# A decoder layer with its tile places and its instruction orders written out as tables

## The chip, the core and the metric

The kernel runs on one core of one Trainium2 chip. The metric is the time on the device in microseconds (us); with a single core, the slowest core is that core. The engines are TensorE (PE in the profile; its weight loads are PEld), VectorE (DVE), ScalarE (ACT), GpSimd (POOL) and SyncE (SP), which only issues loads and stores here.

## The reference

One layer of a hybrid decoder on 512 tokens of width 1024, all in float32:

```python
u = rms_norm(h, ln_mix_pre)
proj = einsum('bsd,de->bse', u, w_in)       # q, k, v of two branches, q of the third, three gates
qa, ka, va, qb, kb, vb, qm, gl = split(proj)
y_swa = swa_sink_attention(qa, ka, va, sinks, rel_bias)   # window 128, 8 heads over 2
y_sb  = stick_breaking_attention(qb, kb, vb)              # 8 heads
y_mem = memory_cross_attention(qm, *split(einsum(rms_norm(mem, ln_mem), w_mem_kv)))  # 256 rows
g = sigmoid(gl)                                           # 3 x 1024
merged = g[0]*(y_swa @ w_branch_swa) + g[1]*(y_sb @ w_branch_sb) + g[2]*(y_mem @ w_branch_mem)
h = h + rms_norm(merged @ w_out, ln_mix_post)
u = rms_norm(h, ln_ffn_pre)
a = silu(u @ w_gate) * (u @ w_up)                         # width 2816
h = h + rms_norm(a @ w_down, ln_ffn_post)
```

## The kernel before

**Products.** Each float32 matrix is split into a high and a low part, `hi` and `lo`. The split is one copy on ScalarE (L137) and one subtraction on VectorE (L138), in `split`; a product is then three matmuls, hi x hi, hi x lo and lo x hi (`mm3`, L169 to L171). The large projections also use a scheme with seven block products p1 to p7 in place of eight. Its sums of weight blocks are made while they are loaded: a first plain load from SyncE fills a tile, and a second load, issued on GpSimd, accumulates into it (`q_issue`, L446, for the gates; `g_plus`, L1224, for gate/up; `dn_issue`, L1364 and L1367, for the down projection). The splits of the weights wait for these loads.

**Streams.** Two objects of class `Stream` hold the work of TensorE as a list of units, `dn` up to the branches and `fs` for the feed-forward part. A unit is one load of weights, one split and a row of matmuls (24 of 256 columns in a gate/up unit). When a unit begins, `ahead` writes the load for four or five units further on and the split for three further on; attention, softmax, gates and norms are written between the pieces of the stream, by their estimated times.

**What sets the order.** The source writes the instructions in that order, but what each engine's queue holds in the end is decided by the scheduler of the Tile framework, which moves instructions past each other on an engine by its own model of when their inputs are ready. Some edges are pinned by `after`, which adds a dependency without a semaphore: all functions of one ScalarE table behind the table's load (`fn`, `table`), the splits behind the copies of `q_end`, and the splits, factors and joins of the first gate/up units behind each other (`behind`, `ordered`). The first stage alone is written under a manual schedule. Each engine then takes its queue in order.

**Where tiles live.** The SBUF and PSUM buffers come from pools that turn round: `ckp` with 73 tiles of 128 x 512 float32, `sm` with 16 small ones, `wp` with four each of raw, hi and lo weight tiles of 128 x 1024, `cst` for constants. PSUM has eight banks, two in pool `psd` and six in `psa`. At the end of the branches `wp` and `cst` are closed and the pool `fp`, with nine load buffers and four hi and lo tiles each, takes their room.

**Places that the prediction speaks of.** They are these, in order of time:
- `q_end` (L540): when the products of a gate's block are ready in PSUM, ScalarE copies the bank out, for p1, p5, p6 and p7, and the bank is used again. The tile is `gq2p` for the third gate (MEM).
- `out_load` and `out_split`: the sixteen 256 KB pieces of `w_out` are loaded on SyncE into tiles `wo00` to `wo17` (L1067, two per step of the loop over `outs`), and split on ScalarE and VectorE into `wo00h` and so on.
- `turn` and `place`: the normalized rows are transposed in PSUM (`pt`), and the right-hand factors B11, B21, T1, N2, N22, T3 and T4 of the gate/up products are written from them (`place`, L1153 and L1154). For the first two row tiles `turn` also keeps a copy of both halves, `ur` (L1171).
- `dn_issue`: the loads of the down projection's weights. For p3 a tile `bp` is loaded for each k (L1372), and for p7 another load accumulates into it on GpSimd (L1367).
- `dn_half` (its last lines L1400 to L1409) and `rstd_small` (L1078 to L1083): the last norm, on each half row of the output, and the stores.

Of the kernel before, what the change touches and what calls it, by code (L numbers as in the profile page):

```python
# [2 lines left out]

# [1 line left out]

# [12 lines left out]
P = 128  # L18
# [10 lines left out]
SPLIT_AHEAD = 3  # L29
QM_FIRST = 3  # L30
WARM = 10


class Stream:
# [70 lines left out]

@with_exitstack
def tile_kernel(ctx, tc, a):
    nc = tc.nc

    base = ctx.enter_context(tc.tile_pool(name="base", bufs=1))  # L110
    ckp = ctx.enter_context(tc.tile_pool(name="ckp", bufs=73))
    sm = ctx.enter_context(tc.tile_pool(name="sm", bufs=16))
    psd = ctx.enter_context(tc.tile_pool(name="psd", bufs=2, space=bass.MemoryType.PSUM))
    psa = ctx.enter_context(tc.tile_pool(name="psa", bufs=6, space=bass.MemoryType.PSUM))
    drm = ctx.enter_context(tc.tile_pool(name="drm", bufs=1, space=bass.MemoryType.DRAM))

    first = ExitStack()
    wp = first.enter_context(tc.tile_pool(name="wp", bufs=4))
    cst = first.enter_context(tc.tile_pool(name="cst", bufs=1))

    def ck(name, dt=F32):
        return ckp.tile([P, 512], dt, tag="ck", name=name)

    def small(name, n=4):
        return sm.tile([P, 8], F32, tag="s", name=name)[:, :n]

    def dps(name):
        return psd.tile([P, 512], F32, tag="d", name=name)

    def aps(name):  # L130
        return psa.tile([P, 512], F32, tag="a", name=name)

    st = {}

# [10 lines left out]

    def w_load(src, n):
        uid[0] += 1
        raw = wp.tile([P, 1024], F32, tag="raw", name=f"raw{uid[0]}")
        nc.sync.dma_start(raw[:, :n], src)
        return raw  # L150

    def w_split(raw, n):
        uid[0] += 1
        hi = wp.tile([P, 1024], F32R, tag="hi", name=f"hi{uid[0]}", bufs=4)
        lo = wp.tile([P, 1024], F32R, tag="lo", name=f"lo{uid[0]}", bufs=4)
# [51 lines left out]


    def const(name, shape, pool=cst):
        t = pool.tile(shape, F32, name=f"c_{name}")  # L210
# [5 lines left out]
    ones = cst.tile([P, P], F32, name="ones")  # L216
    nc.vector.memset(ones[:, :], 1.0)

    def rsqrt(r, v, t, ss):
# [8 lines left out]
    def rstd_of(name, acc, n, bank):  # L228


        if acc.shape[1] > n:
            nc.gpsimd.tensor_tensor(acc[:, :n], acc[:, :n], acc[:, n : 2 * n], op=ALU.add)
        ps = bank(f"ss_{name}")
        mm(ps[:, :n], ones[:, :], acc[:, :n], True, True)
        rb = cst.tile([P, n], F32, name=f"rb_{name}")
# [5 lines left out]
        rs = cst.tile([P, n // P], F32, name=f"rs_{name}")  # L241
        nc.gpsimd.dma_start(rs[:, :], row[:, :].rearrange("o (t p) -> (o p) t", p=P))
        return rs, rb

# [96 lines left out]

        return gen

    v_all = cst.tile([P, NT * 640], F32, name="v_all")

    def own_values(t):
        return v_all[:, t * 640 + P : (t + 1) * 640]
# [345 lines left out]
            add_branch(b)  # L693

    xraw = []
    xg = cst.tile([P, 544], F32, name="xg")
    g_pre, g_mem = xg[:, S : S + KC], xg[:, S + KC : S + 2 * KC]
    g_neg = cst.tile([P, KC], F32, name="g_neg")

    def load_x(k0, k1):  # L700
        for k in range(k0, k1):
# [14 lines left out]

    FIRST = 3
    PIECE = ((0, 2), (2, 5), (5, 8))
    raws = [wp.tile([P, 1024], F32, tag="raw", name=f"raw_first{i}") for i in range(FIRST)]
    his = [wp.tile([P, 1024], F32R, tag="hi", name=f"hi_first{i}", bufs=4) for i in range(FIRST)]  # L720
    los = [wp.tile([P, 1024], F32R, tag="lo", name=f"lo_first{i}", bufs=4) for i in range(FIRST)]

    def first_load(eng, p):
        k0, k1 = PIECE[p]
# [4 lines left out]
        sl = slice(PIECE[p][0] * P, PIECE[p][1] * P)  # L729
        split(raws[i][:, sl], his[i][:, sl], los[i][:, sl])  # L730

    with tc.manual_schedule():

        idle = cst.tile([P, 512], BF16, name="idle")
        nc.vector.memset(idle[:, :], 0.0)
        pw = dps("warm")
        for i in range(WARM):
# [42 lines left out]
    pin[:] = [first_table]  # L780

    ident = const("ident", [P, P], base)
    sinks = cst.tile([P, 8], F32, name="sinks")
    nc.sync.dma_start(sinks[:, :], a["sinks"].to_broadcast([P, 8]))

    nmf = const("negm", [P, P])
    identb = cst.tile([P, P], BF16, name="identb")
    nc.gpsimd.tensor_copy(identb[:, :], ident[:, :])
    negm = cst.tile([P, P], BF16, name="negmb")
# [371 lines left out]
    def turn(t, tmp):  # L1161
        pt = [aps(f"ut{t}{h}") for h in range(2)]
        for h in range(2):
            for k in range(4):
                nc.tensor.transpose(pt[h][:, k * P : (k + 1) * P], tmp[h][:, k * P : (k + 1) * P], ident[:, :])
        turned[t] = pt
        if t < 2:
            turned[t] = [ck(f"ur{t}{h}") for h in range(2)]
            for h in range(2):
                place(("B11", "B21")[h], t, pt[h])  # L1170
                nc.scalar.copy(turned[t][h][:, :], pt[h][:, :])  # L1171
# [24 lines left out]

    HF = NFF // 2
    NCH = (HF + 1) // 2
    aq = {(i, j): [ck(f"aq{i}{j}{c}") for c in range(NCH)] for i in range(2) for j in range(2)}
    sq = [ck(f"sq{c}") for c in range(NCH)]  # L1200
    sr = [ck(f"sr{c}") for c in range(NCH)]

    PROD = ("p1", "p5", "p6", "p3", "p7", "p2", "p4")
    AHEAD_A = 3
# [12 lines left out]

    def g_raw(n, key, i, j):
        uid[0] += 1
        gw[(n, key)] = fp.tile([P, 1024], F32, tag="raw", name=f"gw{uid[0]}")  # L1220
        nc.sync.dma_start(gw[(n, key)][:, :], g_src(n, i, j))

    def g_plus(n, key, i, j):
# [117 lines left out]
    keep = {}  # L1341
    out1 = {}
    gain_out = []
    ssd = [small(f"ssd{t}", 2) for t in range(NT)]
    held = []

    def wsrc(j, h, k):
# [5 lines left out]
    def dn_issue(p, c):  # L1353

        j, h = {"p1": (0, 0), "p5": (0, 1), "p6": (1, 1), "p3": (1, 1), "p7": (0, 1), "p2": (1, 0), "p4": (1, 0)}[p]
        ks = tiles_of(c)
        if p in ("p1", "p5", "p4"):
            n = 512 * len(ks)
            src = a["w_dn"][:, h, j * HF + ks[0] : j * HF + ks[-1] + 1].rearrange("p k n -> p (k n)")
            if p == "p1":  # L1360
                rr[c] = fp.tile([P, 1024], F32, tag="raw", name=f"r{c}")
                nc.sync.dma_start(rr[c][:, :n], src)
            else:
                nc.gpsimd.dma_start(rr[c][:, :n], src, accum_op=ALU.add)  # L1364
        elif p == "p7":
            for k, t in zip(ks, rb[("p3", c)]):
                nc.gpsimd.dma_start(t[:, :], wsrc(j, h, k), accum_op=ALU.add)  # L1367
# [101 lines left out]
    gpost = bcast("g_post")  # L1469
    gfpre = bcast("g_fpre")  # L1470
    dn.until(f"branch{MEM}")
    first.close()
    fp = ctx.enter_context(tc.tile_pool(name="fp", bufs=9, reuse_waits="tile"))

    def f_split(raw, n):
        uid[0] += 1
        hi = fp.tile([P, 1024], F32R, tag="hi", name=f"hi{uid[0]}", bufs=4)
        lo = fp.tile([P, 1024], F32R, tag="lo", name=f"lo{uid[0]}", bufs=4)
# [18 lines left out]
    def load_at(i, fn, *args):  # L1497
        fs.units[i]["load"].append(lambda: fn(*args))
# [26 lines left out]
    def go(to):  # L1525
        while fs.at < to:
            fs.piece()
# [43 lines left out]
    go(len(seq))  # L1571
    table("natural_log_exp_and_others")
    go(len(fs.units))


def _buckets():
# [86 lines left out]
```

## Time and profile before

| what | before |
|---|---|
| median of 3 runs | 788.07 us (787.36 to 788.13) |
| the profiled execution | 787.54 us |
| its span | 785.7 us |
| instructions in it | 12,335 |
| busy PE / DVE / ACT / POOL | 776.3 / 595.4 / 469.3 / 123.2 us |
| granted clock of TensorE | 0.999 |
| moved by DMA | 128.61 MB, 164 GB/s |

The time of an execution is a little longer than its span, here by 1.8 us, which lies before the first and behind the last instruction that the profile counts. Busy time is the time in which an engine executes an instruction. TensorE's matmuls overlap, so one has a busy time longer than the distance to the next. A window is a stretch of the span; the wait view adds up the idle time of an engine by what ended it. In a row of the timeline stand the start, the duration, the engine, the line, the operation with what it writes and reads, and in brackets the idle time before it with what ended that.

### The profile page before, as it was taken

To read this page: it belongs to the slowest core of one execution; us is meant where nothing else is said; L and a number is where in the kernel's file an instruction comes from. 1 tells how busy PE (TensorE), PEld (TensorE's weight loads), DVE (VectorE), ACT (ScalarE), POOL (GpSimd) and SP (SyncE) were. 2 spreads that over 40 slices of the span, in tenths; PEclk is the share of its full clock that TensorE was granted. 3 is DMA by queue.
4 is the path that set the end of the run, shared out by engine and by line. 5 is a ranking of instruction groups with operands and counts; after the bars stand their busy time and mean duration, and the time that the engine had idled before them with its cause. 6 is when DMAs were issued, how large, how long until landed. Compare 5 with 4: busy or idle time off the path is not lost.

```text
span 785.7 us, 12335 instructions
## 1 busy us (share of the span) xinstructions
PE 776.3 (99%) x4638; PEld 682.2 (87%) x4638; DVE 595.4 (76%) x942; ACT 469.3 (60%) x837; POOL 123.2 (16%) x142
## 2 busy tenths in 40 slices
PE   9999999999999999999999999999999999999996
PEld 6899887788888888887888899999999999888885
DVE  6995876686877757876855599867677777898797
ACT  7663676686577666657633577455554455666673
POOL 0203400002011111321261000100000000215200
PEclk9999999999999999999999999999999999999999
DMA  8444923265449794369849418987666651949802
GB/s 301 132 138 121 314 88 108 81 190 124 89 100 206 178 208 139 54 170 250 304 162 255 92 47 219 260 220 191 186 180 183 186 155 54 222 107 239 184 1 108
DMA packets 44220, 128.61 MB, mean 164 GB/s; under 512 B 5248, under 2 KB 6832, under 8 KB 44160
## 3 DMA queue, kind: packets, MB, share of 16 engines
q1 hardware_dynamic: 30480, 85.21, 32.8%
q0 software_dynamic: 13248, 42.22, 27.8%
q8 instruction: 36, 0.59, 0.3%
q10 hardware_dynamic: 432, 0.39, 0.1%
q14 instruction: 24, 0.20, 0.1%
HBM read 120.98 MB, written 4.72 MB: 160 GB/s over the span
## 4 chain that ended last, share of the span: by engine, by line
PE 93%; DMA 2%; DVE 2%; issue 1%; ACT 1%; POOL 0%; DVEq 0%; SPq 0%; ACTq 0%; POOLq 0%
PE gx L169 5%; PE gx L171 5%; PE gx L170 5%; PE gy L171 3%; PE gy L169 3%; PE gy L170 3%; PE x L171 3%; PE x L170 3%; PE x L169 3%; PE br L169 2%; PE br L170 2%; PE br L171 2%; PE mx L171 2%; PE mx L170 2%; PE mx L169 2%; PE g1p L169 2%
## 5 line engine op out<-in xcount | busy, mean ns | idle before, releaser
L137 ACT CAST hi<-gw 128x1024 fp32r<-128x1024 f32 x77 | 79.9, 1048 | 92.7 <-DVE gw L1242 39.6
L138 DVE TENSOR_TENSOR lo<-raw,hi 128x1024 fp32r<-128x1024 f32 (+2 forms) x82 | 99.9, 1219 | 46.2 <-ACT hi L137 45.7
L138 DVE TENSOR_TENSOR lo<-gw,hi 128x1024 fp32r<-128x1024 f32 x77 | 93.5, 1223 | 36.2 <-ACT hi L137 36.2
L137 ACT CAST hi<-raw 128x1024 fp32r<-128x1024 f32 (+2 forms) x82 | 85.2, 1042 | 43.4 <-PE pv L171 13.0
L1224 POOL DMA_DIRECT2D gw<-in_w_gu x27 | 23.3, 883 | 196.4 <-DMA gw<-in_w_gu 91.3
L870 DVE TENSOR_TENSOR_SCAN bw<-br,bw 128x512 f32<-128x512 f32 (+3 forms) x32 | 24.4, 808 | 17.0 <-ACT bw L194 17.0
L137 ACT CAST hi<-r 128x1024 fp32r<-128x1024 f32 (+1 forms) x24 | 23.6, 982 | 19.8 <-PE y L171 5.3
L446 POOL DMA_DIRECT2D raw<-in_w_g x24 | 20.7, 862 | 93.2 <-DVE lo L138 74.2
L170 PE MATMUL x<-lo,lh 128*128 128x512 f32 x88 | 34.2, 389 | 0.0
L169 PE MATMUL x<-hi,lh 128*128 128x512 f32 x88 | 34.2, 389 | 0.0
L171 PE MATMUL x<-hi,ll 128*128 128x512 f32 x88 | 34.1, 389 | 0.0
L138 DVE TENSOR_TENSOR lo<-r,hi 128x1024 fp32r<-128x1024 f32 (+1 forms) x24 | 27.1, 1130 | 3.7 <-ACT hi L137 3.6
L137 ACT CAST hi<-bp 128x512 fp32r<-128x512 f32 x33 | 19.3, 620 | 13.4 <-PE y L171 4.8
L138 DVE TENSOR_TENSOR lo<-bp,hi 128x512 fp32r<-128x512 f32 x33 | 22.7, 721 | 6.0 <-ACT hi L137 5.8
L169 PE MATMUL gx<-B11h,hi 128*128 128x256 f32 x88 | 25.1, 285 | 0.2 <-ACT B11h L1153 0.2
L169 PE MATMUL gx<-T4h,hi 128*128 128x256 f32 x88 | 25.0, 285 | 0.0
L169 PE MATMUL gy<-N22h,hi 128*128 128x256 f32 x88 | 25.0, 284 | 0.0
L171 PE MATMUL gy<-N22h,lo 128*128 128x256 f32 x88 | 25.0, 284 | 0.0
L171 PE MATMUL gw<-B21h,lo 128*128 128x256 f32 x88 | 25.0, 284 | 0.0
L170 PE MATMUL gx<-B11l,hi 128*128 128x256 f32 x88 | 25.0, 284 | 0.0
L170 PE MATMUL gw<-B21l,hi 128*128 128x256 f32 x88 | 24.9, 283 | 0.0
L169 PE MATMUL gy<-T1h,hi 128*128 128x256 f32 x88 | 24.9, 283 | 0.0
(824 smaller groups left out, 2758.7 us busy)
## 6 DMA issues: line engine op xcount, KB each, us to landing
gw<-in_w_gu SPq DMA_DIRECT2D x57, 512.0 KB, 4.8
gw<-in_w_gu POOLq DMA_DIRECT2D x27, 512.0 KB, 7.5
raw<-in_w_g POOLq DMA_DIRECT2D x24, 512.0 KB, 6.0
raw<-in_w_g SPq DMA_DIRECT2D x18, 512.0 KB, 3.9
raw<-in_w_p SPq DMA_DIRECT2D x14, 512.0 KB, 4.5
raw<-in_w_brt SPq DMA_DIRECT2D x12, 512.0 KB, 4.8
bp<-in_w_dn SPq DMA_DIRECT2D x22, 256.0 KB, 10.3
r<-in_w_dn POOLq DMA_DIRECT2D x10, 512.0 KB, 9.1
```

What stands on the lines that cost most here:

```text
L137: ins = nc.scalar.copy(hi, raw)
L138: lows = nc.vector.tensor_tensor(lo, raw, hi.bitcast(F32), op=ALU.subtract)
L169: one = nc.tensor.matmul(out, lh, rh, start=start, stop=False, skip_group_check=True)
L170: nc.tensor.matmul(out, lh, rl, start=False, stop=False, skip_group_check=True)
L171: return one, nc.tensor.matmul(out, ll, rh, start=False, stop=stop, skip_group_check=True)
L446: nc.gpsimd.dma_start(t[:, :], src, accum_op=ALU.add)
L870: st["scan"] = nc.vector.tensor_tensor_scan(x, r, x, 0.0, op0=ALU.mult, op1=ALU.add)
L1224: nc.gpsimd.dma_start(gw[(n, key)][:, :], g_src(n, i, j), accum_op=ALU.add)
```

## The change

The change writes out what the scheduler and the pools decided, as tables in the source.

`ORDER` has a text for each of the five engines, which lists the instructions by their number in the order in which the source issues them ("0-709 716 719 710-715 ..."). A wrapper `Noted` around each engine keeps a list of the instructions that it issued. At the very end each instruction is tied behind the one ahead of it in the table by the dependency without a semaphore that `after` used. `after` itself does nothing while there is a table, and the manual schedule of the first stage is dropped.

`PLAN` has a text for each kind of tile, which lists the number of the buffer that each tile in turn takes. Behind it are tiles that are allocated once: the 73 `ck` tiles, 16 small ones, four raw, hi and lo tiles, and all eight PSUM banks in one kind `p` for `dps` and `aps` alike. The constants lie in one wide tile of 5120 columns, `wide0`, whose five parts of 1024 are later five of the nine load buffers (`fraw`) of the feed-forward stage; the other four are the raw tiles of the first part.

`Late` makes a group of `ck` tiles when they are first asked for, where before all were made ahead. Two places of the work itself move: the copies `ur` of `turn` are issued by `kept`, after both `place` calls and, for the first tile, after `mix(3)`; and the two loads of the tile "t" of the first gate/up row are issued at unit 5 instead of unit 4. The number and the shapes of the instructions stay the same. As all calls pass through the wrapper, the profile of the changed kernel names the wrapper's line for nearly every instruction.

```diff
+ORDER = {
+    "tensor": (
+        "0-709 716 719 710-715 717-718 720-754 761 764 755-760 762-763 765-1098 1106-1109 1099-1105 1110-2246 "
...
+    ),
+    "vector": (
...
+    "scalar": (
...
+    "gpsimd": (
...
+    "sync": (
+        "0-14 16-18 15 19-27 32 28-31 33-34 36-38 35 39-52 57 60 53-56 63-64 58-59 61-62 65-91 94-95 92-93 98-99 "
+        "96-97 100-212"
+    ),
+}
+PLAN = {
+    "raw": (
...
+    "p": (
+        "6 0 5 4 3 2 7 6 1 7 3 0 5 4 2 1 6 7 5 3 0 4 2 1 7 5 0 6 4 2 1 3 6 0 5 4 2 1 7 5 6 4 0 3 2 1 5 7 3 0 5 4 2 "
...
+}
+
+class Noted:
+    def __init__(self, engine):
+        self.engine, self.seen = engine, []
+    def __getattr__(self, name):
+        f = getattr(self.engine, name)
+        def call(*args, **kw):
+            ins = f(*args, **kw)
+            self.seen.append(ins)
+            return ins
+        return call
+
+class Core:
+    def __init__(self, nc):
+        for e in ("tensor", "vector", "scalar", "gpsimd", "sync"):
+            setattr(self, e, Noted(getattr(nc, e)))
+
+class Late:
+    def __init__(self, make):
+        self.make, self.held = make, {}
+    def __getitem__(self, c):
+        if c not in self.held:
+            self.held[c] = self.make(c)
+        return self.held[c]
+
+class Places:
...
+    def take(self, pool, kind, shape, dt, name, **kw):
+        if kind not in PLAN:
+            return pool.tile(shape, dt, tag=kind, name=name, **kw)
+        n = int(next(self.plan[kind]))
+        if kind == "ck":
+            return pool.tile(shape, dt, tag=f"ck{n}", name=name, bufs=1)
+        if kind == "fraw" and n > 3:
+            return self.held["wide0"][:, (n - 4) * 1024 : (n - 3) * 1024]
+        t = self.held[f"{kind.removeprefix('f')}{n}"]
+        return t if dt == F32 else t[:, :].bitcast(dt)
...
-    nc = tc.nc
+    nc = Core(tc.nc)
+    places = Places()
...
-    psd = ctx.enter_context(tc.tile_pool(name="psd", bufs=2, space=bass.MemoryType.PSUM))
     psa = ctx.enter_context(tc.tile_pool(name="psa", bufs=6, space=bass.MemoryType.PSUM))
+    psd = psa if PLAN else ctx.enter_context(tc.tile_pool(name="psd", bufs=2, space=bass.MemoryType.PSUM))
...
     def dps(name):
-        return psd.tile([P, 512], F32, tag="d", name=name)
+        return places.take(psd, "p" if PLAN else "d", [P, 512], F32, name)
...
     def after(ins, first):
+        if not ORDER:
+            follow(ins, first)
+
+    def follow(ins, first):
         dep = mybir.DependencyInfo(mybir.DependencyClass.NoSync, mybir.DependencyReason.DATA)
         tc.add_manual_dep(ins.ins, first.ins.name, dep, reason="order")
...
-    with tc.manual_schedule():
+    with nullcontext() if ORDER else tc.manual_schedule():
...
-    fac = {r: [(ck(f"{r}h{c}", F32R), ck(f"{r}l{c}", F32R)) for c in range(2)] for r in RIGHT}
+    fac = {r: Late(lambda c, r=r: (ck(f"{r}h{c}", F32R), ck(f"{r}l{c}", F32R))) for r in RIGHT}
...
         if t < 2:
-            turned[t] = [ck(f"ur{t}{h}") for h in range(2)]
             for h in range(2):
                 place(("B11", "B21")[h], t, pt[h])
-                nc.scalar.copy(turned[t][h][:, :], pt[h][:, :])
+            st[("kept", t)] = pt
             return
...
+    def kept(t):
+        turned[t] = [ck(f"ur{t}{h}") for h in range(2)]
+        for h in range(2):
+            nc.scalar.copy(turned[t][h][:, :], st[("kept", t)][h][:, :])
...
-    first.close()
-    fp = ctx.enter_context(tc.tile_pool(name="fp", bufs=9, reuse_waits="tile"))
+    if PLAN:
+        fp = None
+    else:
+        first.close()
+        fp = ctx.enter_context(tc.tile_pool(name="fp", bufs=9, reuse_waits="tile"))
...
-    load_at(4, g_raw, 0, "t", 1, 0)
-    load_at(4, g_plus, 0, "t", 0, 0)
+    load_at(5, g_raw, 0, "t", 1, 0)
+    load_at(5, g_plus, 0, "t", 0, 0)
...
     turn(0, tmp[0])
     fs.ahead(5, 3)
     tmp[3] = mix(3)
+    kept(0)
     turn(1, tmp[1])
+    kept(1)
...
+    for e, text in ORDER.items():
+        seen, last = getattr(nc, e).seen, None
+        for part in text.split():
+            a, _, b = part.partition("-")
+            for k in range(int(a), int(b or a) + 1):
+                if last is not None:
+                    follow(seen[k], seen[last])
+                last = k
```

More of the change, by code (lines that the diff above doesn't have):

```diff
@@ L1 @@
 import math
-from contextlib import ExitStack
+from contextlib import ExitStack, nullcontext
 import numpy as np
@@ new lines, with __init__, open, fixed @@
+class Places:
+    def __init__(self):
+        self.plan = {kind: iter(text.split()) for kind, text in PLAN.items()}
+        self.held, self.used = {}, 0
+    def open(self, pool, kind, n, shape):
+        for i in range(n if PLAN else 0):
+            key = f"{kind}{i}"
+            self.held[key] = pool.tile(shape, F32, tag=key, name=key, bufs=1)
+    def fixed(self, pool, shape, dt, name):
+        if not PLAN:
+            return pool.tile(shape, dt, name=name)
+        n = shape[1] if dt == F32 else shape[1] // 2
+        t = self.held["wide0"][:, self.used : self.used + n]
+        self.used += n
+        return t if dt == F32 else t.bitcast(dt)
+    def take(self, pool, kind, shape, dt, name, **kw):
[8 more added lines that the diff above has]
+        return t if dt == F32 else t[:, :].bitcast(dt)
@@ L112, in tile_kernel @@
     sm = ctx.enter_context(tc.tile_pool(name="sm", bufs=16))
[L113 removed]
     psa = ctx.enter_context(tc.tile_pool(name="psa", bufs=6, space=bass.MemoryType.PSUM))
+    psd = psa if PLAN else ctx.enter_context(tc.tile_pool(name="psd", bufs=2, space=bass.MemoryType.PSUM))
     drm = ctx.enter_context(tc.tile_pool(name="drm", bufs=1, space=bass.MemoryType.DRAM))
     first = ExitStack()
+    ctx.callback(first.close)
     wp = first.enter_context(tc.tile_pool(name="wp", bufs=4))
+    for kind in ("raw", "hi", "lo"):
+        places.open(wp, kind, 4, [P, 1024])
+    places.open(wp, "wide", 1, [P, 5120])
     cst = first.enter_context(tc.tile_pool(name="cst", bufs=1))
+    places.open(sm, "s", 16, [P, 8])
+    places.open(psa, "p", 8, [P, 512])
     def ck(name, dt=F32):
[L122 removed]
+        return places.take(ckp, "ck", [P, 512], dt, name)
     def small(name, n=4):
[L125 removed]
+        return places.take(sm, "s", [P, 8], F32, name)[:, :n]
     def dps(name):
[L128 removed]
+        return places.take(psd, "p" if PLAN else "d", [P, 512], F32, name)
     def aps(name):
[L131 removed]
+        return places.take(psa, "p" if PLAN else "a", [P, 512], F32, name)
     st = {}
@@ L147, in w_load @@
         uid[0] += 1
-        raw = wp.tile([P, 1024], F32, tag="raw", name=f"raw{uid[0]}")
+        raw = places.take(wp, "raw", [P, 1024], F32, f"raw{uid[0]}")
         nc.sync.dma_start(raw[:, :n], src)
@@ L153, in w_split @@
         uid[0] += 1
-        hi = wp.tile([P, 1024], F32R, tag="hi", name=f"hi{uid[0]}", bufs=4)
-        lo = wp.tile([P, 1024], F32R, tag="lo", name=f"lo{uid[0]}", bufs=4)
+        hi = places.take(wp, "hi", [P, 1024], F32R, f"hi{uid[0]}", bufs=4)
+        lo = places.take(wp, "lo", [P, 1024], F32R, f"lo{uid[0]}", bufs=4)
         if isinstance(raw, list):
@@ L209, in const @@
     def const(name, shape, pool=cst):
-        t = pool.tile(shape, F32, name=f"c_{name}")
+        t = places.fixed(cst, shape, F32, f"c_{name}") if pool is cst else pool.tile(shape, F32, name=f"c_{name}")
         nc.sync.dma_start(t[:, :], a[name])
@@ L215, in tile_kernel @@
     nc.vector.memset(eps_t, EPS)
-    ones = cst.tile([P, P], F32, name="ones")
+    ones = places.fixed(cst, [P, P], F32, "ones")
     nc.vector.memset(ones[:, :], 1.0)
@@ L234, in rstd_of @@
         mm(ps[:, :n], ones[:, :], acc[:, :n], True, True)
-        rb = cst.tile([P, n], F32, name=f"rb_{name}")
+        rb = places.fixed(cst, [P, n], F32, f"rb_{name}")
         v, t = ck(f"v_{name}"), ck(f"t_{name}")
@@ L240, in rstd_of @@
         nc.gpsimd.dma_start(row[:, :], rb[:1, :])
-        rs = cst.tile([P, n // P], F32, name=f"rs_{name}")
+        rs = places.fixed(cst, [P, n // P], F32, f"rs_{name}")
         nc.gpsimd.dma_start(rs[:, :], row[:, :].rearrange("o (t p) -> (o p) t", p=P))
@@ L342, in val @@
         return gen
-    v_all = cst.tile([P, NT * 640], F32, name="v_all")
+    v_all = places.fixed(cst, [P, NT * 640], F32, "v_all")
     def own_values(t):
@@ L695, in tile_kernel @@
     xraw = []
-    xg = cst.tile([P, 544], F32, name="xg")
+    xg = places.fixed(cst, [P, 544], F32, "xg")
     g_pre, g_mem = xg[:, S : S + KC], xg[:, S + KC : S + 2 * KC]
-    g_neg = cst.tile([P, KC], F32, name="g_neg")
+    g_neg = places.fixed(cst, [P, KC], F32, "g_neg")
     def load_x(k0, k1):
@@ L718, in tile_kernel @@
     PIECE = ((0, 2), (2, 5), (5, 8))
-    raws = [wp.tile([P, 1024], F32, tag="raw", name=f"raw_first{i}") for i in range(FIRST)]
-    his = [wp.tile([P, 1024], F32R, tag="hi", name=f"hi_first{i}", bufs=4) for i in range(FIRST)]
-    los = [wp.tile([P, 1024], F32R, tag="lo", name=f"lo_first{i}", bufs=4) for i in range(FIRST)]
+    raws = [places.take(wp, "raw", [P, 1024], F32, f"raw_first{i}") for i in range(FIRST)]
+    his = [places.take(wp, "hi", [P, 1024], F32R, f"hi_first{i}", bufs=4) for i in range(FIRST)]
+    los = [places.take(wp, "lo", [P, 1024], F32R, f"lo_first{i}", bufs=4) for i in range(FIRST)]
     def first_load(eng, p):
@@ L730, in first_split @@
         split(raws[i][:, sl], his[i][:, sl], los[i][:, sl])
-    with tc.manual_schedule():
-        idle = cst.tile([P, 512], BF16, name="idle")
+    with nullcontext() if ORDER else tc.manual_schedule():
+        idle = places.fixed(cst, [P, 512], BF16, "idle")
         nc.vector.memset(idle[:, :], 0.0)
@@ L1219, in g_raw @@
         uid[0] += 1
-        gw[(n, key)] = fp.tile([P, 1024], F32, tag="raw", name=f"gw{uid[0]}")
+        gw[(n, key)] = places.take(fp, "fraw", [P, 1024], F32, f"gw{uid[0]}")
         nc.sync.dma_start(gw[(n, key)][:, :], g_src(n, i, j))
@@ L1343, in tile_kernel @@
     gain_out = []
-    ssd = [small(f"ssd{t}", 2) for t in range(NT)]
+    ssd = Late(lambda t: small(f"ssd{t}", 2))
     held = []
@@ L1360, in dn_issue @@
             if p == "p1":
-                rr[c] = fp.tile([P, 1024], F32, tag="raw", name=f"r{c}")
+                rr[c] = places.take(fp, "fraw", [P, 1024], F32, f"r{c}")
                 nc.sync.dma_start(rr[c][:, :n], src)
```

48 lines of the change are left out of this document (40 added, 8 removed), and 84 rows, old and new, of tables (ORDER, PLAN).

## The prediction

> **What bounds the kernel now.** I read the page first, then the busy time by stage, then who waited for whom on TensorE, then the chain and the timelines of the one stretch that these point to.
>
> ```profile
> span 785.7 us, 12335 instructions
> PE 776.3 (99%) x4638; PEld 682.2 (87%) x4638; DVE 595.4 (76%) x942; ACT 469.3 (60%) x837; POOL 123.2 (16%) x142
> ```
>
> TensorE is busy for 99% of the span. The windows say where the other 9.4 us are:
>
> ```profile
> core 0: us, PE busy (x) PEld busy (x) DVE busy (x) ACT busy (x) POOL busy (x), PEclk, DMA share, GB/s
> 0.00:340.00 340.00, 338.64 (x1812) 282.15 (x1813) 254.91 (x449) 221.36 (x417) 55.99 (x73) 1.00 0.55 150
> 340.00:380.00 40.00, 38.56 (x169) 31.23 (x169) 27.92 (x31) 28.00 (x40) 6.46 (x7) 1.00 0.93 258
> 380.00:449.00 69.00, 69.00 (x326) 57.66 (x325) 40.69 (x76) 27.68 (x65) 22.38 (x19) 1.00 0.70 196
> 449.00:500.00 51.00, 50.84 (x420) 50.23 (x419) 46.63 (x78) 34.41 (x68) 3.44 (x4) 1.00 0.55 150
> 500.00:779.00 279.00, 279.00 (x1917) 260.91 (x1915) 222.32 (x303) 156.69 (x246) 34.90 (x39) 1.00 0.63 162
> 779.00:785.70 6.70, 0.29 (x2) 0.00 (x0) 2.92 (x7) 1.18 (x4) 0.00 (x0) 0.90 0.42 158
> ```
>
> Up to 340 us the only idle time is 1.36 us at the very start. From 340 to 380 it is 1.44 us, from 449 to 500 it is 0.16 us, and after the last matmul 6.4 us of VectorE work and stores remain. At a granted clock of 1.00 the matmuls themselves cannot shrink, since the change keeps their number and shapes. So an order of instructions can win at most about 2 us here, and can lose any amount. The wait view names the idle time:
>
> ```profile
> PE g2p L169 <- ACT gq2p L540: 1.4, 2, 1.0
> PE gx L169 <- ACT B11h L1153: 0.2, 1, 0.2
> ```
>
> Two waits of TensorE on ScalarE's copy of a PSUM bank (`q_end`, the copy of products p5 and p7 for the MEM gate) hold nearly all of it, and the chain shows what was behind each:
>
> ```profile
> 344.73 10.19 DMA raw<-in_w_g
> 355.01 0.67 ACT hi L137
> 355.97 0.59 ACT gq2p L540
> 356.60 0.50 PE g2p L169
> ```
> ```profile
> 372.20 0.96 ACT hi L137
> 373.16 0.48 ACT gq2p L540
> 373.68 0.50 PE g2p L169
> ```
>
> ScalarE takes its instructions in order. The copy at 355.97 stood behind a weight split that waited for an accumulating GpSimd load, 10.19 us on its way. A matmul's busy time is 0.39 us, but the next starts 0.23 us after it:
>
> ```profile
> 349.12 0.39 PE L171 MATMUL g2p<-hi,ul 128*128 128x512 f32 x1
> 349.35 0.39 PE L169 MATMUL g2p<-hi,uh 128*128 128x512 f32 x1
> ```
>
> So each stall costs 0.16 us more than its idle time: 1.0 + 0.16 = about 1.1 us for the first, 0.4 + 0.16 = about 0.6 us for the second.
>
> **The change part by part.** Comparing the two built programs engine by engine gives what the tables do. TensorE's 4,572 instructions keep their order but for 52, all among the first gate/up units (the stage at 449 us). SyncE moves 3 of its 213 loads. VectorE has 679 of 942 instructions in another place, ScalarE 496 of 768, GpSimd 73 of 145. No instruction is added or removed.
>
> *ScalarE between 345 and 356 us* is the part that matters. Before:
>
> ```profile
> 350.02 0.72 ACT L194 ACTIVATE gq2p<-gq2p,rs_x 128x512 f32<-128x512 f32 x1 [0.93 <-DVE gq2p L543]
> 350.65 1.04 ACT L137 CAST hi<-raw 128x1024 fp32r<-128x1024 f32 x1
> 351.75 0.73 ACT L194 ACTIVATE gq2p<-gq2p,rs_x 128x512 f32<-128x512 f32 x1
> 355.01 1.05 ACT L137 CAST hi<-raw 128x1024 fp32r<-128x1024 f32 x1 [2.54 <-DMA raw<-in_w_g]
> 355.97 1.06 ACT L540 COPY gq2p<-g2p 128x512 f32<-128x512 f32 x2
> 357.37 1.05 ACT L137 CAST hi<-raw 128x1024 fp32r<-128x1024 f32 x1 [0.34 <-DMA raw<-in_w_g]
> 358.33 0.61 ACT L137 CAST wo10h<-wo 128x512 fp32r<-128x512 f32 x1
> ```
> ```profile
> 363.32 0.62 ACT L137 CAST wo02h<-wo 128x512 fp32r<-128x512 f32 x1
> 363.85 0.62 ACT L137 CAST wo03h<-wo 128x512 fp32r<-128x512 f32 x1
> ```
>
> The changed table puts wo10h, wo11h, wo02h and wo03h, which stood behind that copy, ahead of it: the order is wo00h, wo01h, a split, wo10h, wo11h, wo02h, wo03h, the split of 350.65, the two sigmoids, the split of 355.01, and only then the copy of p5. Queued behind wo03h's wait for its load are thus four instructions and the copy that TensorE needs. That load is the last of six that SyncE issues at 342.9 to 345.3 us, and the change moves none of them. The first fence is the last of them alone, the second the one before it, the third the queues while it was on its way:
>
> ```profile
> wo<-in_w_out SPq DMA_DIRECT2D x1, 256.0 KB, 9.8
> ```
> ```profile
> wo<-in_w_out SPq DMA_DIRECT2D x1, 256.0 KB, 5.6
> ```
> ```profile
> DMA packets 311, 0.88 MB, mean 252 GB/s; under 512 B 26, under 2 KB 26, under 8 KB 309
> q0 software_dynamic: 148, 0.56, 80.9%
> q1 hardware_dynamic: 161, 0.30, 25.3%
> ```
>
> It was issued at 345.3 and landed at 355.1 us, because from 349.5 to 353.0 us the accumulating loads of GpSimd (q0) took 80.9% of the engines' time. Before, nobody noticed: wo03h was read at 363.85. Now ScalarE waits for it. The loads leave about 0.3 us earlier, since small waits near 131 and 139 us go with the new order of the stick-breaking copies, so I take 354.8. Then come wo03h (0.53, start to start, 363.32 to 363.85), the split (0.96, 357.37 to 358.33), two sigmoids (0.63 each, 350.02 to 350.65), the second split (0.96, 355.01 to 355.97), and the copy until TensorE starts (0.63, 355.97 to 356.60): 4.3 us. TensorE goes on at 359.1 instead of 356.6 us: **+2.5**. TensorE's arrival does not enter, as it waits in both.
>
> When the load lands is the unknown, so it has bounds. Equal turns between the two queues would give it twice the undisturbed spacing, and this batch's spacing is about 0.6 us (1.2 us after the 350.4 of its predecessor: 351.6). A quarter of the engines' time gives 350.4 + 0.6/0.25 = 352.8. The row itself gives 354.8, and a start of q0 relative to the six loads that shifts by a few tenths gives up to 355.5. I take the row: same loads, same queue, same rivals for the engines. [...]
>
> *The second stall.* With TensorE 2.5 us later, ScalarE's copy of p7 is ready in time, as what is ahead of it (splits whose loads were issued long before) was not held by TensorE: **-0.6**, bounds -0.6 and 0.
>
> *The gate/up start.* In the new order the first matmuls of gate/up unit 1 come sooner, and their bank is freed by the copies that `kept` now places behind both `place` calls:
>
> ```profile
> 451.60 1.08 ACT L1171 COPY ur<-ut 128x512 f32<-128x512 f32 x2
> ```
>
> One copy is 0.54 us; TensorE meets about half of it: +0.2, bounds 0 and 0.5. Against it stands the 0.16 us of small waits in this window, which the new VectorE order may remove: together **+0.1**.
>
> *The end.*
>
> ```profile
> 780.05 0.69 DVE fg L1406
> 780.74 0.08 DVE v_d L1080
> ```
>
> The table puts v_d ahead of the fg product, so it runs while ScalarE makes r_d: **-0.2**.
>
> *At nothing.* The PSUM pool of 8 instead of 2 + 6, the numbered SBUF places, the constants in one tile that later holds five load buffers, the late allocation, and the two loads of "t" one unit later change only which earlier reader a writer waits for. What hides them is that splits run three units ahead, and a unit of 24 matmuls is 24 x 0.23 = 5.5 us; the windows with 69.00 of 69.00 and 279.00 of 279.00 us show that cover holding. Where it goes, the cost is one split, 1 to 2 us.
>
> Sum: 2.5 - 0.6 + 0.1 - 0.2 = **+1.8 us**. The profiled execution took 787.54 us for a span of 785.7, and would take 789.3. The median of the runs is 788.07, 0.5 above it, so the forecast is 788.07 + 1.8 = **789.9 us**, slower by 0.23%. A measurement of this kernel tells about 0.2% (1.6 us) from no change, so this is close to that border.
>
> **Rivals.** *wo03 lands early* (not slower). If the six loads keep their spacing, or take equal turns, wo03 is there by 351.6, ScalarE is through the sigmoids by 354.4, and the copy hangs on the accumulating load again, 0.3 us earlier than before: -0.4 - 0.6 + 0.1 - 0.2 = -1.1, 787.0 us. It decides from a landing before about 353.0 us, where the 4.3 us end early enough that the sum is zero. For it speaks the 5.6 us of the load just ahead of it in the queue; against it the 9.8. [...] Chance 0.15.
>
> *TensorE never waits* (faster). If the accumulating loads also land earlier, both stalls go: -1.1 - 0.6 - 0.2 - 0.2 = -2.1, 786.0 us. Nothing in the profile shows why they should. Chance 0.07.
>
> *The down stage's accumulating loads* (slower still). GpSimd's table issues the accumulation for tile 7 of the last third product six places early and that for tile 6 behind it, and the latter waits for the former's semaphore.
>
> ```profile
> L1367 POOL DMA_DIRECT2D bp<-in_w_dn x2: 859/859/859, 722.4 to 723.4; - x2
> DMA to landing us min/median/max: 14.4/14.9/15.5
> 736.94 0.62 ACT L137 CAST hi<-bp 128x512 fp32r<-128x512 f32 x1 [1.42 <-PE x L170]
> ```
>
> These are the two. If tile 7 leaves some 8 us before its 722.4 (an estimate: six places earlier, when its buffer is free) and takes 15.5, tile 6 leaves behind it at about 730.5 and with 14.4 lands at 744.9; its split ends 0.6 later, 1.1 us after TensorE needs it. Together +2.9: 791.0 us. Against it: the queue serves in order, and these 14 us are mostly the time behind others, so a lane freed sooner gives the rest back. Chance 0.15.
>
> *It does nothing*: the tables repeat what the scheduler had wherever it matters, and 788.1 us stays. For it speak TensorE's and SyncE's orders, against it ScalarE's. Chance 0.13.
>
> **How the numbers follow.** The forecast has 0.50. Its landing between 354.0 and 355.5 gives +1.0 to +2.5, of which some two thirds lie over 1.6 us: 0.34 slower, 0.16 within. The down stage adds 0.15 slower. Within 0.2% are also wo03 early (0.13 of its 0.15) and nothing (0.13). Faster has 0.07 + 0.02. So 0.09, 0.42, 0.49. The range goes from 786.9, just under the early landing, to 791.6, just over the down stage's case, and leaves out the case without any wait and the upper tails.
>
> **What would show it.** In the changed profile ScalarE's wo03h near 354 us should end an idle time of 2 us or more "<-DMA wo", followed by split, two sigmoids, split and copy; TensorE's wait on the gq2p copy should be one of some 3.5 us instead of two of 1.4 together; the window 340 to 380 should hold some 3.5 us of idle time and 500 to 779 none. All recorded instructions will carry one line number, so tiles must be read. The prediction is wrong if wo03 lands before 353 us, if TensorE waits near 744 us, or if idle time shows up in a stage where it has none now.

## The result

The changed kernel takes 791.86 us (median of 22 runs, 787.63 to 794.76) where the kernel before takes 788.00 (22 runs, 787.32 to 789.43): a ratio of 1.0045, 95% interval 1.0034 to 1.0056. By the ratio it is slower by 0.45%, by the medians by 3.9 us, and its runs are spread over 7 us instead of 2.

The page of its profiled execution (793.13 us, span 791.4), first lines:

```profile
span 791.4 us, 12326 instructions
PE 777.5 (98%) x4638; PEld 684.2 (86%) x4638; DVE 598.8 (76%) x942; ACT 468.7 (59%) x837; POOL 127.8 (16%) x142
```

TensorE's busy time grows by 1.2 us, though its matmuls are the same, and the rest of the 5.7 us of span is idle time. The windows, with the columns of before:

```profile
0.00:340.00 340.00, 338.60 (x1817) 282.93 (x1818) 257.78 (x450) 220.26 (x417) 59.04 (x74) 1.00 0.56 150
340.00:380.00 40.00, 33.99 (x138) 27.59 (x137) 21.59 (x23) 21.95 (x30) 5.54 (x7) 0.91 0.80 192
...
449.00:500.00 51.00, 50.83 (x400) 49.32 (x399) 43.59 (x75) 33.29 (x71) 3.44 (x4) 1.00 0.50 140
500.00:779.00 279.00, 279.00 (x1939) 262.02 (x1938) 226.81 (x306) 159.90 (x245) 36.66 (x39) 1.00 0.66 162
```

Of these only 340 to 380 us is different: 6.01 us idle instead of 1.44, and the granted clock 0.91 instead of 1.00. The wait view has one wait there, where it had two:

```profile
PE p L181 <- ACT gq2p L181: 6.0, 1, 6.0
PE p L181 <- ACT B11h L181: 0.2, 1, 0.2
```

ScalarE's timeline shows what the copy of p5 (the COPY, which now takes two tiles) stood behind:

```profile
348.60 0.62 ACT L181 CAST wo10h<-wo 128x512 fp32r<-128x512 f32 x1 [0.20 <-DMA wo<-in_w_out]
350.25 0.62 ACT L181 CAST wo11h<-wo 128x512 fp32r<-128x512 f32 x1 [1.04 <-DMA wo<-in_w_out]
353.49 0.62 ACT L181 CAST wo02h<-wo 128x512 fp32r<-128x512 f32 x1 [2.61 <-DMA wo<-in_w_out]
356.33 0.62 ACT L181 CAST wo03h<-wo 128x512 fp32r<-128x512 f32 x1 [2.23 <-DMA wo<-in_w_out]
356.86 1.04 ACT L181 CAST hi<-raw 128x1024 fp32r<-128x1024 f32 x1
357.80 1.33 ACT L181 ACTIVATE gq2p<-gq2p,wide 128x512 f32<-128x512 f32 x2
359.04 1.03 ACT L181 CAST hi<-raw 128x1024 fp32r<-128x1024 f32 x1
359.98 1.05 ACT L181 COPY gq2p<-p 128x512 f32<-128x512 f32 x2
```

Four copies in a row end an idle time on a load of `w_out`. The last load took 12.0 us, in the issue view, and TensorE stood from its last matmul to the next:

```profile
wo<-in_w_out SPq DMA_DIRECT2D x1, 256.0 KB, 12.0
```
```profile
354.20 0.39 PE L181 MATMUL p<-hi,xsp51l 128*128 128x512 f32 x1
360.60 0.80 PE L181 MATMUL p<-hi,xsp30h 128*128 128x512 f32 x1 [6.01 <-ACT gq2p L181]
361.19 0.63 PE L181 MATMUL p<-lo,xsp30h 128*128 128x512 f32 x1
361.62 0.63 PE L181 MATMUL p<-hi,xsp30l 128*128 128x512 f32 x1
```

Behind the wait a matmul takes 0.63 us instead of 0.39 and the next starts 0.43 us later instead of 0.23. The windows of the wait and of the time after it say why:

```profile
354.40:360.60 6.20, 0.19 (x1) 0.00 (x0) 3.10 (x5) 4.27 (x7) 0.86 (x1) 0.94 0.44 88
360.60:366.50 5.90, 5.90 (x14) 4.70 (x15) 2.12 (x2) 1.70 (x3) 1.72 (x2) 0.50 0.98 168
```

The granted clock is 0.50 for 5.9 us. Laying the starts of the same matmul in both traces side by side (the order on TensorE is the same up to the gate/up stage) gives the balance of this execution: 1.0 us ahead of before up to the wait, +5.0 at the wait, +2.8 for the half clock, -0.8 at the second wait, which is gone, -0.2 in the first gate/up units, -0.2 behind the last matmul. That is +5.6 us, the 785.7 and 791.4 of the two spans. The median moved less, by 3.9.

### The profile page after: what moved, and what is told of

Same layout as the page of the kernel before. It is cut to its first block, busy times and chain, and to the rows that moved or that the text cites. A ratio compares the mean times of both kernels' runs of the same rounds, so it can differ in the third digit from the quotient of the medians.

```text
span 791.4 us, 12326 instructions
## 1 busy us (share of the span) xinstructions
PE 777.5 (98%) x4638; PEld 684.2 (86%) x4638; DVE 598.8 (76%) x942; ACT 468.7 (59%) x837; POOL 127.8 (16%) x142
## 4 chain that ended last, share of the span: by engine, by line
PE 54%; ACT 0%; DVE 0%; issue 0%; DVEq 0%
PE p L181 54%; DVE fg L181 0%; ACT mt L181 0%; DVEq L1889 0%; DVE s L181 0%; ACT gq2p L181 0%; ACT B11h L181 0%; ACT sqr L181 0%
## 5 line engine op out<-in xcount | busy, mean ns | idle before, releaser
L181 DVE TENSOR_TENSOR lo<-raw,hi 128x1024 fp32r<-128x1024 f32 (+4 forms) x139 | 162.6, 1175 | 76.2 <-ACT hi L181 75.7
L181 ACT CAST hi<-raw 128x1024 fp32r<-128x1024 f32 (+4 forms) x139 | 137.8, 996 | 117.1 <-PE p L181 67.5
L181 DVE TENSOR_TENSOR lo<-wide,hi 128x1024 fp32r<-128x1024 f32 x53 | 64.5, 1221 | 20.3 <-ACT hi L181 20.3
L181 ACT CAST hi<-wide 128x1024 fp32r<-128x1024 f32 x53 | 55.6, 1050 | 37.7 <-PE p L181 16.0
L181 PE MATMUL p<-lo,lh 128*128 128x512 f32 x154 | 59.9, 389 | 0.0
L181 PE MATMUL p<-hi,lh 128*128 128x512 f32 x154 | 59.9, 389 | 0.0
L181 PE MATMUL p<-hi,ll 128*128 128x512 f32 x154 | 59.7, 389 | 0.0
L181 PE MATMUL p<-hi,uh 128*128 128x512 f32 (+1 forms) x160 | 57.2, 358 | 0.0
L181 PE MATMUL p<-lo,uh 128*128 128x512 f32 (+1 forms) x160 | 57.1, 357 | 0.0
L181 PE MATMUL p<-hi,ul 128*128 128x512 f32 (+1 forms) x160 | 57.1, 357 | 0.0
```

The source lines that it names most:

```text
L181: ins = f(*args, **kw)
```

## The experiments

Each kernel was timed in five rounds against the kernel before. The ratio, with its interval, is taken over the runs and need not equal the quotient of two medians. All but wo_early build on the changed source.

### window_old: the old order in one stretch

```diff
 ORDER["scalar"]:
-375 374 379-380 376 386-387 390-391 377-378 381-385 388-389
+375 374 379-380 376 378 377 381-391
 ORDER["vector"]: the 13 entries behind 424, in the order of the kernel before
```

(376, 377, 382, 385, 388, 389 are weight splits, 378 and 381 sigmoids, 383 and 384 the p5 copies, 386, 387, 390 and 391 are wo10h, wo11h, wo02h, wo03h.)

> The changed kernel, with ScalarE's and VectorE's order of the kernel before in one stretch alone (around the copy of p5 of the third gate), so that wo10h, wo11h, wo02h and wo03h stand behind that copy again. Theory A (the four copies of w_out pieces ahead of the gq2p copy are the whole loss): TensorE's wait at that copy falls from 6.0 to under 1.5 us and its clock stays at 1.00 in 340 to 380 us; as TensorE reached the place about 1 us earlier than before, 786.5 to 787.5 us. Rival B (the fixed places, or the other moved instructions, among them GpSimd's earlier accumulating loads, cost it): the wait stays above 3 us and the time at 790 or more.

785.04 us (784.69 to 785.52), ratio 0.9958 (0.9946 to 0.9970): faster than the kernel before, by more than theory A gave. The window, the wait, the loads of `w_out` and ScalarE:

```profile
340.00:380.00 40.00, 39.82 (x176) 32.66 (x175) 29.43 (x33) 30.41 (x43) 5.81 (x7) 1.00 0.96 269
```
```profile
PE p L180 <- ACT gq2p L180: 0.2, 1, 0.2
```
```profile
DMA to landing us min/median/max: 4.1/6.1/11.9
```
```profile
353.44 1.05 ACT L180 CAST hi<-raw 128x1024 fp32r<-128x1024 f32 x1 [2.10 <-DMA raw<-in_w_g]
354.40 1.13 ACT L180 COPY gq2p<-p 128x512 f32<-128x512 f32 x2
...
362.67 0.62 ACT L180 CAST wo03h<-wo 128x512 fp32r<-128x512 f32 x1
```

The slowest load of `w_out` still takes 11.9 us; wo03h at 362.67 does not notice. Of the two waits of the kernel before, 1.4 us together, only 0.2 us is left, which theory A had not counted on. So 13 places in ScalarE's table and as many in VectorE's turn the changed kernel from 3.9 us slower into 3.0 us faster.

### wo_early: the new order of the four copies, without any table

```diff
     for i, (h, q) in enumerate(outs):          # the kernel before
-        out_load(h, q)
+        if i == 0:
+            for x in outs[:3]:
+                out_load(*x)
+        elif i > 2:
+            out_load(h, q)
         dn.run(2.6)
...                                             # out_split the same
```

> The kernel before, without tables, with its scheduler and its pools; only the source asks for the first six pieces of w_out and their splits together, which puts the copies wo10h, wo11h, wo02h and wo03h ahead of the p5 copy on ScalarE. Theory A: TensorE waits 3 to 7 us at that copy, and the time is 790.5 to 794 us. Rival B (the tables or the places are needed for the loss): 787.5 to 788.5 us.

790.58 us (788.77 to 794.68), ratio 1.0037 (1.0023 to 1.0052). TensorE waits for the same copy, behind the same load:

```profile
PE g2p L169 <- ACT gq2p L540: 5.4, 1, 5.4
```
```profile
359.48 0.62 ACT L137 CAST wo03h<-wo 128x512 fp32r<-128x512 f32 x1 [2.57 <-DMA wo<-in_w_out]
360.01 1.06 ACT L540 COPY gq2p<-g2p 128x512 f32<-128x512 f32 x2
```
```profile
360.64:363.60 2.96, 2.96 (x7) 2.38 (x8) 1.41 (x2) 1.38 (x2) 0.03 (x1) 0.50 0.70 138
```

The copies ahead of the p5 copy are enough: neither tables nor fixed places are needed for the loss, its spread (5.9 us here) or the half clock.

### narrow_p6: GpSimd's accumulating loads, nearly gone

```diff
+        if (b, p) == (MEM, "p6"):
+            nc.gpsimd.dma_start(t[:, :16], src[:, :16], accum_op=ALU.add)
```

> The changed kernel with its order as it is; the accumulating GpSimd loads of the third gate's p6 bring 16 of their 1024 columns, so two transfers of 512 KB are nearly gone from 344 to 356 us and that part of the weights is left out. Contention theory (wo03's load is late because GpSimd's accumulating loads take most of the DMA engines' time): wo03 lands before 352.5 us, TensorE's wait at the copy is under 1 us, and the time is 785.5 to 787.5 us. Rival (the load is late by itself, behind the five ahead of it in its queue): it lands after 354 us, the wait stays above 3 us, the time near 791.

784.65 us (784.18 to 785.42), ratio 0.9954 (0.9941 to 0.9967), with the changed order.

```profile
DMA to landing us min/median/max: 4.0/5.6/6.4
```
```profile
350.70 0.62 ACT L181 CAST wo03h<-wo 128x512 fp32r<-128x512 f32 x1 [0.29 <-DMA wo<-in_w_out]
```
```profile
PE p L181 <- ACT gq2p L181: 0.3, 1, 0.3
```

This kernel leaves out most of two weight loads, so only its time and its trace count. The same six loads of `w_out` land within 6.4 us, wo03h runs at 350.70, and the loss is gone. Like window_old it took less than expected, with 0.3 us left of the wait.

### halves: the same bytes in shorter packets

```diff
+        cut = (0, 512, 1024) if (b, p) == (MEM, "p6") else (0, 1024)
+        for x, y in zip(cut, cut[1:]):
+            nc.gpsimd.dma_start(t[:, x:y], src[:, x:y], accum_op=ALU.add)
```

> The changed kernel with its order; each of the two accumulating GpSimd loads of the third gate's p6 is issued as two loads of 512 columns, so its packets carry 2 KB instead of 4 KB and the bytes are the same. If the DMA engines take turns packet by packet between the two queues, whatever a packet's length (by the rows of 349.5 to 353 us a packet of GpSimd's took 0.31 us and one of SyncE's 0.09 us): a turn gets shorter, wo03 lands 1.5 to 4 us earlier than the 356.3 us of the changed kernel's profile, TensorE's wait falls to 2 to 4.5 us, and the time is 786.5 to 790 us. Rival (the share of the time goes by bytes, or by the queue): wo03 lands no earlier than 355.5 us, and the time is 791 to 793.

787.15 us (785.79 to 790.16), ratio 0.9994 (0.9983 to 1.0005). The queues from 349 to 353 us, first in the changed kernel, then here, and here the slowest load of `w_out` and the wait:

```profile
q0 software_dynamic: 182, 0.68, 85.4%
q1 hardware_dynamic: 159, 0.29, 21.8%
```
```profile
q0 software_dynamic: 315, 0.58, 82.0%
q1 hardware_dynamic: 197, 0.34, 26.8%
```
```profile
DMA to landing us min/median/max: 4.4/5.1/8.1
```
```profile
PE p L181 <- ACT gq2p L181: 2.1, 1, 2.1
```

16 engines by 4 us make 64 us: a packet of GpSimd's queue took 0.854 x 64 / 182 = 0.30 us, and with half the columns 0.82 x 64 / 315 = 0.17; one of SyncE's 0.09 both times. SyncE's queue got 197 packets through instead of 159, and wo03 took 8.1 us instead of 12.0. So the packets' length matters here, as the expectation had it. Strict turns, one packet for one, would make the two counts equal while both queues have work, and from 350 to 351 us they are: 60 and 60 here, 39 and 41 in the changed kernel. Over four microseconds they are not (315 and 197, 182 and 159). From 352 to 353 us SyncE's queue has 10 packets here beside 112; that it had too little work left by then is my reading. In the changed kernel four of its last eight 2 KB packets start about 0.40 us apart (353.43, 353.83, 354.24 and 354.64 us), which is about the 0.30 and 0.09 us of one packet from each queue. So the end of wo03 fits one packet per turn; that the engines work in such turns is not shown beyond these counts and distances. The records do not name the DMA engine of a packet, so that one engine had fallen behind the others is not shown either.

### three_ahead: one copy fewer ahead

```diff
 ORDER["scalar"]: 391 (wo03h) behind 385; ORDER["vector"]: 433 (its subtraction) behind 427
```

> The changed kernel; of the four copies only wo03h (with its subtraction) goes back behind the copies of p5, so ScalarE waits for wo02's load instead, which landed near 353.5 us in the changed kernel's profile. Theory A (the wait is the landing of the last piece ahead plus the 4.3 us of ScalarE's work behind it): TensorE goes on near 357.8 us, a wait of 3 to 4 us, and if its clock stays at 1.00 the time is that of window_old plus about 3: 787.5 to 788.7 us. If the clock falls after an idle time of this length as it did after 6.0 us, 1 to 3 us more: up to 791. Rival (the four pieces land together, whichever is waited for): no less than 790.5, with a wait of over 5 us.

785.68 us as the median of runs from 784.54 to 792.57, ratio 0.9994 (0.9970 to 1.0017): unclear. Seven of the twelve runs lie below 786.1, the others at 788.1 to 792.6. In those five the mean granted clock is 0.994 to 0.996, in the seven 0.997 to 0.999; none of the five was profiled. The profiled run was of the first kind:

```profile
350.93 0.62 ACT L181 CAST wo02h<-wo 128x512 fp32r<-128x512 f32 x1 [0.96 <-DMA wo<-in_w_out]
```
```profile
PE p L181 <- ACT gq2p L181: 0.6, 1, 0.6
```

The same load let wo02h start at 353.49 in the changed kernel and at 350.93 here, early enough for TensorE. My expectation took one landing for all runs, and was wrong in that; the rival's "no less than 790.5" fell too.

### busy_wait and busy_24: TensorE kept busy inside the wait

```diff
+                for _ in range(36 if (b, p, c, i) == (MEM, "p3", 0, 0) else 0):
+                    mm(places.held["p2"][:, :P], ident[:, :], ident[:, :], True, True)
```

> The changed kernel with its order; 36 matmuls of 128 columns on the identity, into a PSUM bank that nothing uses then, stand ahead of the matmul that waits for the p5 copy, so that TensorE has about 4 us of work inside the wait of 6 us. If the idle time is what halves TensorE's clock behind the wait: the clock stays at 1.00 from 360 to 367 us, and the time is about 2.6 us below the changed kernel's, 788.5 to 789.8 us. If the clock falls for another reason (the DMA load there, or the time of the run): it is 0.5 again behind the wait and the time is 791 to 793 us.

792.44 us (792.11 to 792.55), ratio 1.0052 (1.0035 to 1.0069). I had sized the work wrongly; the profile counts two matmuls for each of the 36:

```profile
354.45 7.97 PE L181 MATMUL p<-c_ident 128*128 128x128 f32 x70
```

They outlast the wait, so the time lies in the rival's range, but the granted clock is 1.00 from 354 to 366 us, as it should be if the idle time halves it. With 24 of them:

> As busy_wait with 24 instead of 36 matmuls on the identity. In busy_wait one took 0.22 us, so that the 36 lasted from 354.45 to 362.4 us, about 2.2 us beyond the copy that TensorE waits for; 24 end near 359.8. If the half clock is what the idle time costs: the clock stays at 1.00, TensorE goes on near 360, and the time is 789.3 to 790.5 us, below the changed kernel by 1 to 2.5. If the idle time that is left (under 1 us) or something else still halves the clock: 791.5 us or more.

789.71 us (789.36 to 790.85), ratio 1.0029 (1.0018 to 1.0039), by the medians some 2 us below the changed kernel. From the wait on, in two windows:

```profile
354.40:360.00 5.60, 5.60 (x51) 5.56 (x50) 3.36 (x4) 4.96 (x8) 0.86 (x1) 1.00 0.59 101
360.00:367.00 7.00, 7.00 (x33) 5.78 (x33) 2.98 (x4) 2.80 (x3) 1.72 (x2) 1.00 0.98 181
```

The four copies stand where they stood and still wait for their loads (wo02h 2.21 us, wo03h 2.54), and the clock stays at 1.00: TensorE's idle time itself halved it. The spread falls from 7 us (22 runs) to 0.4 and 1.5 (5 and 7 runs), which fits that it comes from the length of this wait and the clock behind it.

### moves_alone: the moves in the source without tables

```diff
-ORDER = { ... }
-PLAN = { ... }
+ORDER = {}
+PLAN = {}
```

> The changed source with both tables empty: pools and scheduler as before, and only the small moves are left (the ur copies behind the place calls, the late allocation, the loads of t one unit later). Theory A (the gain of the other parts, which window_old shows, comes from the tables' order): within 0.1% of before, 787.3 to 788.8 us, with TensorE's small waits near 131 and 140 us and two waits at the gq2p copies still there. Rival (the moves in the source bring it): 785 to 786.5 us.

789.13 us (788.44 to 790.53), ratio 1.0011 (1.0000 to 1.0023).

```profile
PE gx L51 <- ACT B11h L51: 1.4, 1, 1.4
...
PE g2p L51 <- ACT gq2p L51: 1.0, 2, 0.6
PE gx L51 <- DVE b_h L51: 0.4, 1, 0.4
```

That is 0.3 us above what I expected and far from the rival. Without tables the moves bring nothing, and the first gate/up matmul waits 1.4 us for a B11h factor instead of 0.2. What window_old gains is the tables' work. Whether their orders or their places do it was not tried apart.

### copies_first and best: the p5 and p7 copies first

```diff
 ORDER["scalar"] of window_old: 383-384 ahead of 382, 401-402 ahead of 400
```

> As window_old, and the two copies of p5 stand ahead of the split whose accumulating load is late, the two copies of p7 ahead of the split before them. If the copies alone hold TensorE: no wait of TensorE on a gq2p copy is left, 785.0 to 786.5 us and below window_old by 0.6 to 1.8 us. Rival (TensorE then waits for that split itself, or VectorE's part of it): a wait on hi or lo of 0.5 to 1.5 us takes its place, and the time is that of window_old.

785.47 us (785.17 to 786.28), ratio 0.9965 (0.9951 to 0.9979): within the expected times, but not below window_old. No wait on ScalarE's gq2p copies is left, and another one is there, on VectorE:

```profile
PE p L181 <- DVE gq2p L181: 1.0, 1, 1.0
```
```profile
396.40 1.22 DVE L181 TENSOR_TENSOR lo<-raw,hi 128x1024 fp32r<-128x1024 f32 x1 [5.59 <-ACT hi L181]
397.54 0.68 DVE L181 TENSOR_TENSOR gq2p<-p,gq2p 128x512 f32<-128x512 f32 x1
```

The cause is the same once more: an operation that frees a PSUM bank, queued behind the split of a load that is late. Neither theory had this wait. With the two splits put behind:

```diff
 ORDER["scalar"]: 443, 456 (splits) behind 421; ORDER["vector"]: 500, 519 behind 464
```

> As copies_first, and the splits of the first two gate/up weights stand behind the four mgh copies on ScalarE, and behind the copy of the last gate product and the four mgl on VectorE, so that TensorE's wait near 397 us (1.0 us on a VectorE copy that stood behind the split of a late load) has no cause. If so: 1.1 us below copies_first, 784.0 to 784.8 us, and below window_old. Rival: the late splits are then missed at the start of gate/up, a wait near 450 us of 0.5 us or more, and the time stays at 785.0 to 785.6.

784.64 us (784.54 to 784.77), ratio 0.9954 (0.9937 to 0.9971). The waits near 355, 373 and 397 us are gone:

```profile
340.00:380.00 40.00, 40.00 (x178) 33.02 (x178) 27.09 (x30) 28.01 (x40) 6.13 (x7) 1.00 0.95 266
380.00:449.00 69.00, 68.83 (x333) 57.61 (x332) 43.70 (x82) 28.80 (x72) 23.00 (x19) 1.00 0.70 191
```

It is faster than both the kernel before and the changed one. Against window_old (785.04, measured on another chip) the difference of 0.4 us lies within the two intervals.

## Why the prediction was right in its mechanism and short in its sizes

- *The place and the mechanism* held: wo03h ends an idle time of 2.23 us on its load, then come split, two sigmoids, split, copy, and one wait of TensorE takes the place of two. The 4.3 us from wo03h to TensorE's start were 356.33 to 360.60, 4.27. window_old and wo_early show that these copies are the loss.
- *The landing* was the term that was mis-sized. I took the row of 9.8 us and 354.8; it took 12.0 and came at 356.3, though issued 1.0 us earlier and not 0.3. My bounds ended at 355.5. The step at fault: one row was taken as the value of a load that varies by microseconds from run to run (9.5 us in best, 9.8 before, 9.9 in three_ahead, 11.9 in window_old and 14.6 in wo_early, beside the same accumulating loads).
- *Equal turns* was misread. I let the two queues share the time equally, which gave 351.6 and which no run shows; the quoted rows already said that a packet of GpSimd's took 0.809 x 56 / 148 = 0.31 us against 0.253 x 56 / 161 = 0.09. What the changed kernel's trace shows from 350 to 351 us is equal counts, 39 and 41 packets, and with these times of a packet SyncE's queue then has about a quarter of the time (0.09 of 0.40 us), which is the 25.3% of the row and the case of 352.8. By 353 us most of the load was indeed through; its last packets, four of them about 0.40 us apart, went on until 356.0. So equal counts spoke for a late landing, not for the rival to which I gave 0.15.
- *The clock* had no term at all: "At a granted clock of 1.00 the matmuls themselves cannot shrink" left out that they can grow. A wait of 6 us cost 2.8 more.
- *TensorE's lead* was put at 0.3 us and was 1.0: 0.4 at 131 and 140 us as said, 0.3 near 207 us (the transposes between two matmuls of a branch), and 0.25 in the first 9 us. Part of it may vary between executions: wo_early, without tables, began its last matmul of p5 at 354.85 us, the kernel before at 355.24. It does not help where the wait's end is set by a load.
- *The second wait*, -0.6, was -0.8; the first gate/up units, +0.1, were -0.2 (+0.3 at the bank, -0.5 behind it, near 473 and 487 us); the end, -0.2, was -0.2. *At nothing* held: the window 500 to 779 us has 279.00 of 279.00, and the down stage's rival did not occur. What I held against that rival, that GpSimd's queue serves in order, is what the trace of before shows of that place: its eleven accumulating loads issued from 714.5 to 730.8 us landed in the order of their issue, from 724.8 to 743.1 us, 1.3 to 2.2 us apart.
- *TensorE never waits* got 786.0 us and "nothing in the profile shows why" the other loads should land earlier. window_old is that case, at 785.0: the split ahead of its copy started at 353.44 instead of 355.01.

So the sum of +1.8 us stands beside +3.9 in the medians and +5.6 in the profiled execution. The way and the path were forecast; that the range reached as far as the result is luck. By the ratio the result is 788.07 x 1.0045 = 791.6 us, just the upper end, and that end had been set for the down stage's case, which did not occur. The forecast's own case ended at +2.5, 790.6 us.

## What to carry to other kernels

When an order is frozen by hand, look on each engine for the operations that free a PSUM bank for TensorE, and let nothing stand ahead of them that waits for a load in flight: an early place for work that nobody needs yet was no gain here, and it tied TensorE to the slowest load of its batch (12.0 us, a wait of 6.0). Price such a wait by the worst landing that the traces show (14.6 us here), not by one row, and add what the clock takes after the idle time (2.8 us here). A wider spread between runs (7 us here, instead of 2) can be a sign that the chain now runs through a DMA.

## What the runs showed of the hardware

TensorE's clock fell to half around the end of a stall in the middle of a full kernel in three of the traces, and for how long did not follow the stall's length: 6.0 us idle was followed by 5.9 us at 0.50, and 5.4 us idle (wo_early) by 3.0. In the kernel with shorter packets (halves) 2.1 us idle was enough; its matmuls went on at full speed for 1.3 us and then fell back:

```profile
357.30:358.90 1.60, 1.50 (x6) 1.28 (x7) 1.09 (x2) 1.48 (x3) 0.30 (x1) 0.94 0.92 123
358.90:363.00 4.10, 4.10 (x12) 3.16 (x12) 1.16 (x2) 1.05 (x1) 1.42 (x2) 0.61 1.03 195
```

The 1.0 us idle in the kernel before left it at 1.00. In the clock records of the traces the half clock lasts 3.41 us in halves and in wo_early and 6.83 us, twice that, in the changed kernel, where it begins at 359.85 us, before TensorE goes on at 360.60. So 2.1 and 5.4 us idle were followed by the same 3.41 us. What sets the moment of the fall and its length, and how much idle time is enough between 1.0 and 2.1 us, these runs do not show.
